# A decoder layer's RWKV recurrence: the inverse from its last row up, Pool's large operations on VectorE and ACT, the decay moved into the state update

## The chip, the core and the metric

The kernel runs on one core of a Trainium2 chip. Its engines work side by side, each through its own list of instructions in order: PE (TensorE, matrix products), DVE (VectorE), ACT (ScalarE), POOL (GpSimd) and SP, which here only issues DMAs. The metric is the device time of one execution in microseconds (us), lower is better.

## The reference

One step of one decoder layer for 512 prompt tokens and 8 sample tokens (520 columns, 2048 channels). What matters here is the RWKV-7 branch, a recurrence over time with one 64x64 state per head:

```python
kk = hd(k.astype(f32) * k_k)
kk = kk / jnp.maximum(jnp.sqrt(jnp.sum(kk * kk, axis=-1, keepdims=True)), 1e-12)
kf = hd(k.astype(f32) * (1.0 + (a - 1.0) * k_a))
...
def step(S, inp):
    r_t, w_t, k_t, v_t, a_t, b_t = inp
    sa = jnp.einsum('bhij,bhj->bhi', S, a_t)
    S = S * w_t[:, :, None, :] + sa[..., None] * b_t[:, :, None, :] + v_t[..., None] * k_t[:, :, None, :]
    return S, jnp.einsum('bhij,bhj->bhi', S, r_t)
...
S, o = _wkv7_scan(wkv_prev, rf, hd(decay), kf, vf, -kk, kk * hd(a))
```

`o` is normalised per head, a bonus term is added, and the sum is gated by `silu(gate_a)`. Beside it stands a convolution branch (31 taps, layer norm, its own gate). Both are projected, merged by sigmoid gates, projected again and normalised. All weights and activations are float32.

## The kernel before

**Matrix products.** Each large product takes its 128x512 weight block as a high and a low part: ACT copies the block rounded to `wh` (line 154), DVE subtracts, `wl = w - wh`, and PE runs three products of 260 columns for each half of the tokens (`step`, line 195; line 211). Four k-steps share one block, that is 24 matmuls. `wh` and `wl` have four buffers each, and a block is prepared three blocks ahead (`AHEAD`).

**The recurrence** is done in chunks of 64 tokens, for two heads (128 channels) at a time: eight passes of `wkv(p, box)`, p = 0 to 7. One pass has these stages:
- the prelude: `kk`, `b`, `kf` (kept in the tile named `a`), the bonus factor `rk`, its high part `hi`, the bonus `bv`, the decays `ep` and `em` (the latter in the tile `cs`), and the products `ar` and `bk` with them;
- the inverse: a 32x32 triangular matrix for each of 32 blocks, brought into `ni` through DRAM (`nd`), is inverted row by row, 31 times a multiply into `tm` and a sum into `ti`, both on DVE; the result goes through DRAM (`td`) into `tts`, DVE transposes a part of it to `d` (the program's `d11`), and two sets of small products on PE with `yt` between them complete the 64x64 inverse in `ttb`;
- the loop over 8 chunks: PE makes `aux`, ACT copies it to `xs`, PE multiplies by `ttb`, ACT copies to `suv`, PE multiplies by `bkt` (the transposed `bk`), and DVE makes the next state from `sf` and the chunk's decay `epl`; four k-steps of the large products stand between two such stages;
- the end: normalisation (`m`, `o`, `on`), `og`, and a DMA to `oa_d`.

The convolution of the same number (`conv(i, u)`: 30 multiply-adds of some 500 columns into `c` on DVE) runs after the inverse.

**Order.** The program writes PE's order, and for this part DVE's too. The stages above are generators that are advanced one tick after each k-step of a large product (`tick`, line 181). `yield n` waits n ticks. `yield ROOM` lets a stage go on only while a running sum of DVE's planned work is no more than 1 us ahead of PE's planned work. The sum charges a DVE instruction of n elements 0.14 + 0.00107 n us and a large Pool instruction 0.0007 n us; ACT's work is not charged. ACT, POOL and SP are ordered by the scheduler.

Nearly all DVE and POOL instructions are issued by one helper, so the profile gives them line 67; they are told apart by their tiles.

Of the kernel before, what the change touches and what calls it, by code (L numbers as in the profile page):

```python
# [70 lines left out]
def body(nc, tc, a):  # L71
    with ExitStack() as es:
# [356 lines left out]
        def wkv(p, box):  # L429
# [67 lines left out]
            yield 2
# [11 lines left out]
            ar = [kq.tile([P, NCH, 2, 64], F32, name=f"ar{h}", bufs=2) for h in range(2)]
            bk = kq.tile([P, NCH, 2, 64], F32, name="bk")  # L510
            for h in range(2):
                s = half(h)
                yield ROOM
                tt(vec, ar[h][s, :, h, :], ch(kk)[s], ep[s, :, 0:64], ALU.mult)
                tt(gps, ar[h][s, :, 1 - h, :], ch(r)[s], ep[s, :, 1:65], ALU.mult)
# [2 lines left out]
                tt(gps, bk[s, :, 1 - h, :], ch(kf)[s], ch(em)[s], ALU.mult)
# [37 lines left out]
            gps.tensor_copy(epl, ep[:, :, 64])  # L556
            tt(gps, bh, bh, ep[:, :, 64:65].to_broadcast([P, NCH, P]), ALU.mult)
            ni = kq.tile([P, 32, 32], F32, name="ni")
            for g in range(4):
# [4 lines left out]
            gps.tensor_scalar(ti.rearrange("p i t -> p (i t)"), ttinit, 1.0, 0.0, op0=ALU.mult, op1=ALU.add)
            yield 3
            for t in range(1, 32):
                tm = kq.tile([P, 8, 32], F32, name="tm")
                tt(vec, tm[:, :, :t + 1], ti[:, :, :t + 1],
                   ni[:, 0:t + 1, t].unsqueeze(1).to_broadcast([P, 8, t + 1]), ALU.mult)
                vec.tensor_reduce(ti[:, :, t], tm[:, :, :t + 1], axis=AX.X, op=ALU.add)  # L570
                yield ROOM
            flag["inv"] = p
            for g in range(4):
                dma(out=td.rearrange("h c e i t -> (h c e) i t")[:, g * 8:(g + 1) * 8, :], in_=ti[g * 32:(g + 1) * 32])
            for h in range(2):
                for e in range(2):
                    dma(out=tts[h * 64 + e * 32:h * 64 + e * 32 + 32, :, e * 32:e * 32 + 32],
                        in_=td[h, :, e].rearrange("c i t -> i c t"))
            yield 16
            for h in range(2):  # L580
# [19 lines left out]
            for c in range(NCH):  # L600
                for h in range(2):
                    x, y = quarter(2 * h), quarter(2 * h + 1)
                    pe.matmul(o[x, c, 0:32], lhsT=yt[y, c, :], rhs=tts[y, c, 32:64], start=True, stop=True)
            for h in range(2):
                s = half(h)
                gps.tensor_scalar(ttb[s, :, s], tts[s], 1.0, 0.0, op0=ALU.mult, op1=ALU.add)
# [21 lines left out]
            yield 7  # L628

            oc = aux("oc").rearrange("p (c x) -> p c x", x=64)  # L630
            sf = kq.tile([P, 64], F32, name="sf", bufs=2)
            gps.memset(sf, 0.0)
            for c in range(NCH):
                x = aux().rearrange("p (c x) -> p c x", x=64)
                for h in range(2):
                    pe.matmul(x[half(h), 0, :], lhsT=ar[h][:, c, h, :], rhs=suv[:, h, c, :], start=True, stop=True)
                for h in range(2):
                    pe.matmul(oc[half(h), c, :], lhsT=ar[h][:, c, 1 - h, :], rhs=suv[:, h, c, :], start=True, stop=False)
                xs = kq.tile([P, 64], F32, name="xs", bufs=2)
                act(xs, x[:, 0, :], AF.Copy)  # L640
                yield ly
                pe.matmul(x[:, 2, :], lhsT=ttb[:, c, :], rhs=xs, start=True, stop=True)
                for h in range(2):
                    act(suv[half(h), h, c, :], x[half(h), 2, :], AF.Copy)
# [42 lines left out]
            og = gt("og")[:, :NPR]  # L687
# [25 lines left out]
        def conv(i, u):  # L713

            yield 8
            sc = kp.tile([P, NS, 31], F32, name="sc")
# [13 lines left out]
            act(c[:, :NPR], u[:, :NPR], AF.Identity, scale=cw[:, 30:31], bias=col(O_CB, i))  # L730
# [400 lines left out]
```

## Time and profile before

| | |
|---|---|
| median of 3 runs | 1838.17 us (1833.41 to 1839.06) |
| the profiled execution's own time | 1836.85 us |
| its span, first to last instruction | 1835.1 us |
| PE busy | 1785.5 us (97%) |
| DVE busy | 1279.5 us (70%) |
| ACT busy | 743.3 us (41%) |
| POOL busy | 353.3 us (19%) |

The shares are means over a span whose stages differ: the eight passes of the recurrence fill about the first 1100 us, and what follows is the rest of the large products. `PEclk` is the clock that TensorE was granted, as a share of full speed. In a timeline, a number in square brackets is the idle time of the engine just before that instruction, with what ended it.

### The profile page before, as it was taken

Reading aid. Unit: us, or ns where it says so; the run is one execution under the profiler, and the core shown is the slowest. Engines: PE = TensorE matmul, PEld = TensorE weight load, DVE = VectorE, ACT = ScalarE, POOL = GpSimd, SP = SyncE. Lnnn points to the kernel's source line nnn. Section 1 sums busy time; section 2 is a strip of 40 time slices with the busy share of each in tenths; the row PEclk is TensorE's granted clock in tenths of the full one; section 3 lists DMA queues with packets and bytes.
Section 4 is the critical chain, followed back from the end, with each engine's and each line's share of the span. In section 5 each row is a group of like instructions: output and inputs, shape, how many; then the busy total and the mean of one; then the engine's idle time right before and its main releaser. Section 6 shows DMA issues by size and latency. Waiting matters only on the chain.

```text
span 1835.1 us, 37880 instructions
## 1 busy us (share of the span) xinstructions
PE 1785.5 (97%) x15576; PEld 1744.7 (95%) x15576; DVE 1279.5 (70%) x2300; ACT 743.3 (41%) x1355; POOL 353.3 (19%) x370
## 2 busy tenths in 40 slices
PE   9999999999999999999999999999999999999996
PEld 9999999999998999989999999999999999999995
DVE  6569999799798797896996998465444333334456
ACT  6735336244253363353362332454333222243354
POOL 1222203113113013032131155001022000011102
PEclk9999999999999999999999999999999999999998
DMA  6252322532432433324323344467555433362232
GB/s 232 84 133 79 107 93 79 114 92 74 119 103 68 112 96 98 96 80 107 94 84 104 122 131 149 130 225 238 192 179 185 123 116 98 93 195 93 93 104 94
DMA packets 121037, 220.49 MB, mean 120 GB/s; under 512 B 47888, under 2 KB 56208, under 8 KB 120864
## 3 DMA queue, kind: packets, MB, share of 16 engines
q1 hardware_dynamic: 119264, 216.47, 38.4%
q8 instruction: 122, 2.00, 0.4%
q10 hardware_dynamic: 1600, 1.60, 0.3%
q14 instruction: 51, 0.42, 0.1%
HBM read 188.69 MB, written 29.34 MB: 119 GB/s over the span
## 4 chain that ended last, share of the span: by engine, by line
PE 74%; DVE 19%; issue 3%; ACT 1%; POOL 1%; DMA 1%; SPq 0%; DVEq 0%; ACTq 0%; POOLq 0%
PE mm L211 68%; PE aux L67 5%; DVE wl L67 4%; DVE tm L67 4%; DVE c L67 3%; DVE ti L67 2%; PE aux L211 1%; DVE p L67 1%; DVE sq L67 1%; DVE on L67 1%; PE oc L67 1%; DMA w<-in_win 0%; DVE h L67 0%; DVE suv L67 0%; DVE m L67 0%
## 5 line engine op out<-in xcount | busy, mean ns | idle before, releaser
L154 ACT ACTIVATE wh<-w 128x512 fp32r<-128x512 f32 (+1 forms) x541 | 338.7, 628 | 627.5 <-PE mm L211 503.8
L211 PE MATMUL mm<-xh,wh 128*128 128x260 f32 x2784 | 589.1, 293 | 0.4 <-ACT xh L266 0.4
L211 PE MATMUL mm<-xh,wl 128*128 128x260 f32 x2784 | 565.9, 285 | 4.6 <-DVE wl L67 4.6
L211 PE MATMUL mm<-xl,wh 128*128 128x260 f32 x2784 | 566.0, 285 | 0.3 <-DVE xl L67 0.3
L67 DVE TENSOR_TENSOR wl<-w,wh 128x512 fp32r<-128x512 f32 (+1 forms) x541 | 397.5, 738 | 200.4 <-ACT wh L154 198.3
L211 PEld LDWEIGHTS mm<-xh,wh 128*128 128x128 f32 x2784 | 432.6, 191 | 12.1 <-ACT wh L154 0.6
L211 PEld LDWEIGHTS mm<-xh,wl 128*128 128x128 f32 x2784 | 433.7, 191 | 5.2 <-DVE wl L67 5.2
L211 PEld LDWEIGHTS mm<-xl,wh 128*128 128x128 f32 x2784 | 433.8, 191 | 0.6 <-DVE xl L67 0.5
L211 PE MATMUL mm<-hi,wl 128*128 128x260 f32 x1600 | 333.5, 284 | 2.6 <-DVE wl L67 2.6
L211 PE MATMUL mm<-hi,wh 128*128 128x260 f32 x1600 | 333.3, 283 | 0.0
L211 PE MATMUL mm<-lo,wh 128*128 128x260 f32 x1600 | 332.4, 282 | 0.0
L211 PEld LDWEIGHTS mm<-hi,wl 128*128 128x128 f32 x1600 | 250.7, 189 | 3.1 <-DVE wl L67 3.1
L211 PEld LDWEIGHTS mm<-hi,wh 128*128 128x128 f32 x1600 | 252.0, 189 | 0.1
L211 PEld LDWEIGHTS mm<-lo,wh 128*128 128x128 f32 x1600 | 251.8, 189 | 0.0
L67 DVE SCALAR_TENSOR_TENSOR c<-u,prm,c 128x482 f32<-128x482 f32 (+14 forms) x240 | 201.6, 840 | 4.4
L67 DVE TENSOR_TENSOR tm<-ti,ni 128x16 f32<-128x16 f32 (+30 forms) x248 | 104.1, 420 | 4.9
L67 POOL TENSOR_TENSOR sq<-hi,lo 128x520 f32<-128x520 f32 (+1 forms) x20 | 24.3, 1220 | 337.8 <-DVE one L67 184.0
L67 DVE TENSOR_TENSOR p<-mm,rs 128x520 f32<-128x520 f32 x78 | 53.7, 689 | 48.3 <-PE mm L211 48.2
L67 DVE TENSOR_REDUCE ti<-tm 128x8 f32<-128x16 f32 (+30 forms) x248 | 73.6, 297 | 8.5
L67 DVE TENSOR_TENSOR s<-mm,s 128x520 f32<-128x520 f32 x32 | 22.4, 700 | 65.9 <-PE mm L211 65.9
L67 POOL COPY nsh<-p 128x9 f32<-128x9 f32 x25 | 14.9, 597 | 238.0 <-DVE p L67 238.0
L67 DVE SCALAR_TENSOR_TENSOR suv<-sf,epl,aux 64x64 f32<-64x64 f32 x112 | 31.1, 278 | 38.4 <-PE aux L67 22.4
(233 smaller groups left out, 1652.5 us busy)
## 6 DMA issues: line engine op xcount, KB each, us to landing
w<-in_win SPq DMA_DIRECT2D x170, 512.0 KB, 3.7
w<-in_wout SPq DMA_DIRECT2D x32, 512.0 KB, 3.7
w<-in_wpg SPq DMA_DIRECT2D x24, 512.0 KB, 3.7
s<-sga_d SPq DMA_DIRECT2D x32, 260.0 KB, 2.8
w<-in_wpa SPq DMA_DIRECT2D x16, 512.0 KB, 3.8
w<-in_wpb SPq DMA_DIRECT2D x16, 512.0 KB, 3.8
wx<-in_wpg SPq DMA_DIRECT2D x32, 256.0 KB, 3.5
x<-in_xT SPq DMA_DIRECT2D x16, 260.5 KB, 5.7
```

What stands on the lines that cost most here:

```text
L67: return f(*args, **kw)
L154: behind.append(act(wh[:, k], w[:, k], AF.Copy))
L211: nc.tensor.matmul(o[h], lhsT=w[:, used[0] % 4, :], rhs=x[:, h * HF:(h + 1) * HF], start=(k == 0 and i == 0), stop=(k == nk - 1 and i == 2))
```

## The change

1. The inverse runs from row 30 up to row 0 and multiplies by `ni[:, t:t+1, t:]`, a row of each matrix, where the old one multiplied by a column `ni[:, 0:t+1, t]`. The result comes out in the other orientation: it is loaded as `dtt`, used by PE directly for the first set of small products, and transposed once on DVE to `dt` for the second.
2. Pool's large operations of the recurrence move. To DVE: the half of `ar` and `bk` that Pool made, the product `kf*k`, the two products of `og` (the first now reads PE's result and applies the scale), and in the convolution the samples' product `tm` and the sum `csum`. To ACT: `kf`'s scale and offset, the bias of `og` (now added to `bv`), `epl`, the initial `ti`, and the copies into `ttb`.
3. The product of all of `bk` with the chunk's last decay (`bh`, 128x1024 on Pool) goes. The decay is applied in the state update instead: DVE makes `suv = aux*epl + sf`, and ACT makes the next `sf` from it by a scale. The separate DVE instruction for `sf` stays for the last chunk only.
4. `og` uses the buffer of `bv`, and `rk` of pass p waits in the program until `og` of pass p-2 was issued (`flag["out"]`).

```diff
-            gps.tensor_scalar(kf, av, col(O_KA, p), oka[:, p:p + 1], op0=ALU.mult, op1=ALU.add)
-            tt(gps, kf, kf, k, ALU.mult)
-            yield 5
+            act(kf, av, AF.Identity, scale=col(O_KA, p), bias=oka[:, p:p + 1])
+            yield 3
+            tt(vec, kf, kf, k, ALU.mult)
+            yield 1
...
+            while p > 1 and flag["out"] < p - 2:
+                yield 1
...
+            act(bv[:, :NPR], bv[:, :NPR], AF.Identity, bias=col(O_LB, p))
...
-                tt(gps, ar[h][s, :, 1 - h, :], ch(r)[s], ep[s, :, 1:65], ALU.mult)
+                yield ROOM
+                tt(vec, ar[h][s, :, 1 - h, :], ch(r)[s], ep[s, :, 1:65], ALU.mult)
...
-            tt(gps, bh, bh, ep[:, :, 64:65].to_broadcast([P, NCH, P]), ALU.mult)
...
-            gps.tensor_scalar(ti.rearrange("p i t -> p (i t)"), ttinit, 1.0, 0.0, op0=ALU.mult, op1=ALU.add)
+            act(ti.rearrange("p i t -> p (i t)"), ttinit, AF.Copy)
...
-            for t in range(1, 32):
+            for t in range(30, -1, -1):
                 tm = kq.tile([P, 8, 32], F32, name="tm")
-                tt(vec, tm[:, :, :t + 1], ti[:, :, :t + 1],
-                   ni[:, 0:t + 1, t].unsqueeze(1).to_broadcast([P, 8, t + 1]), ALU.mult)
-                vec.tensor_reduce(ti[:, :, t], tm[:, :, :t + 1], axis=AX.X, op=ALU.add)
+                tt(vec, tm[:, :, t:], ti[:, :, t:], ni[:, t:t + 1, t:].to_broadcast([P, 8, 32 - t]), ALU.mult)
+                vec.tensor_reduce(ti[:, :, t], tm[:, :, t:], axis=AX.X, op=ALU.add)
...
-                vec.transpose(d11[h * 64:h * 64 + 32], tts[h * 64:h * 64 + 32, :, 0:32])
+            vec.transpose(dt, dtt)
...
-                    pe.matmul(o[y, c, 0:32], lhsT=nba[x, c, 32:64], rhs=d11[x, c, :], start=True, stop=True)
+                    pe.matmul(o[y, c, 0:32], lhsT=nba[x, c, 32:64], rhs=dtt[x, c, :], start=True, stop=True)
...
-                        vec.scalar_tensor_tensor(suv[s, h, c + 1, :], sf[s], epl[s, c:c + 1], x[s, 3, :], op0=ALU.mult, op1=ALU.add)
-                s0 = sf
-                sf = kq.tile([P, 64], F32, name="sf", bufs=2)
-                vec.scalar_tensor_tensor(sf, s0, epl[:, c:c + 1], x[:, 3, :], op0=ALU.mult, op1=ALU.add)
+                        vec.scalar_tensor_tensor(suv[s, h, c + 1, :], x[s, 3, :], epl[s, c:c + 1], sf[s], op0=ALU.mult, op1=ALU.add)
...
+                    act(sf[half(h)], suv[half(h), h, c + 1, :], AF.Copy, scale=epl[half(h), c + 1:c + 2])
...
-            act(og, ot, AF.Identity, scale=col(O_LG, p), bias=col(O_LB, p))
-            tt(gps, og, og, bv[:, :NPR], ALU.add)
-            tt(gps, og, og, sl[:, :NPR], ALU.mult)
+            yield 1
+            vec.scalar_tensor_tensor(og, ot, col(O_LG, p), bv[:, :NPR], op0=ALU.mult, op1=ALU.add)
+            tt(vec, og, og, sl[:, :NPR], ALU.mult)
```

PE's instructions keep their number and sizes, and so do the loads and stores around the inverse (four `td` stores, four loads back). Two places show how the lists move. The first is DVE in the prelude of one pass while the loop of the pass ahead runs; `c` is the convolution, `wl` the weights' low part. Before:

```order
L67 SCALAR_TENSOR_TENSOR kk<-kk,sq 128x520
L67 SCALAR_TENSOR_TENSOR b<-kk,a 128x520
L67 TENSOR_TENSOR wl<-w,wh 128x512
L67 SCALAR_TENSOR_TENSOR c<-u,prm,c 128x505
L67 SCALAR_TENSOR_TENSOR c<-u,prm,c 128x506
L67 SCALAR_TENSOR_TENSOR c<-u,prm,c 128x507
L67 TENSOR_TENSOR wl<-w,wh 128x512
L67 SCALAR_TENSOR_TENSOR rk<-r,prm,a 128x520
```

And now:

```order
L67 SCALAR_TENSOR_TENSOR kk<-kk,sq 128x520
L67 SCALAR_TENSOR_TENSOR b<-kk,a 128x520
L67 SCALAR_TENSOR_TENSOR c<-u,prm,c 128x507
L67 TENSOR_TENSOR wl<-w,wh 128x512
L67 SCALAR_TENSOR_TENSOR c<-u,prm,c 128x508
L67 TENSOR_TENSOR a<-a,k 128x520
L67 SCALAR_TENSOR_TENSOR c<-u,prm,c 128x509
L67 TENSOR_TENSOR wl<-w,wh 128x512
L67 SCALAR_TENSOR_TENSOR rk<-r,prm,a 128x520
```

The product `a*k` stands on DVE between `b` and `rk`, so `rk` waits for nothing on Pool any more. The second place is ACT at the end of an inverse, where the initial `ti` of the next pass is now made. Before, with `ti` on Pool's list:

```order
L674 ACTIVATE m<-m,eps 128x8
L154 ACTIVATE wh<-w 128x512
L154 ACTIVATE wh<-w 128x512
L154 ACTIVATE wh<-w 128x512
L689 ACTIVATE og<-aux,prm 128x512
L382 ACTIVATE q<-p,prm 128x519
L154 ACTIVATE wh<-w 128x512
```

And now:

```order
L679 ACTIVATE m<-m,eps 128x8
L154 ACTIVATE wh<-w 128x512
L154 ACTIVATE wh<-w 128x512
L567 ACTIVATE ti<-cst 128x256
L154 ACTIVATE wh<-w 128x512
L382 ACTIVATE q<-p,prm 128x519
L154 ACTIVATE wh<-w 128x512
```

`ti` may be overwritten only when the four `td` stores of the pass that has just ended have read it, so on ACT the following conversions of weights and the next `q` now stand behind that wait; `og` has left ACT.

More of the change, by code (lines that the diff above doesn't have):

```diff
@@ L408, in lowrank @@
             flag["low"] = True
-        tts = kq.tile([P, NCH, 64], F32, name="tts")
         ttb = kq.tile([P, NCH, P], F32, name="ttb")
         nbrs = [kq.tile([P, NCH, P], F32, name=f"nbr{i}") for i in range(2)]
-        for x in (tts, ttb, *nbrs):
+        for x in (ttb, *nbrs):
             gps.memset(x, 0.0)
-        d11 = kq.tile([P, NCH, 32], F32, name="d11")
-        flag = {"samples": 0, "inv": -1, "done": -1, "loop": -1, "conv": 0, "yp": None, "merged": False}
+        flag = {"samples": 0, "out": -1, "inv": -1, "done": -1, "loop": -1, "conv": 0, "yp": None, "merged": False}
         def firsts(box):
@@ L514, in wkv @@
                 tt(vec, ar[h][s, :, h, :], ch(kk)[s], ep[s, :, 0:64], ALU.mult)
[L515 removed]
+                yield ROOM
+                tt(vec, ar[h][s, :, 1 - h, :], ch(r)[s], ep[s, :, 1:65], ALU.mult)
                 yield ROOM
                 tt(vec, bk[s, :, h, :], ch(b)[s], ch(em)[s], ALU.mult)
[L518 removed]
+                yield ROOM
+                tt(vec, bk[s, :, 1 - h, :], ch(kf)[s], ch(em)[s], ALU.mult)
             for i, x in enumerate((kk, b, kf, r, v)):
@@ L555, in wkv @@
             epl = kq.tile([P, NCH], F32, name="epl", bufs=2)
-            gps.tensor_copy(epl, ep[:, :, 64])
-            tt(gps, bh, bh, ep[:, :, 64:65].to_broadcast([P, NCH, P]), ALU.mult)
+            act(epl, ep[:, :, 64], AF.Copy)
             ni = kq.tile([P, 32, 32], F32, name="ni")
@@ L574, in wkv @@
                 dma(out=td.rearrange("h c e i t -> (h c e) i t")[:, g * 8:(g + 1) * 8, :], in_=ti[g * 32:(g + 1) * 32])
+            dtt = kq.tile([P, NCH, 32], F32, name="dtt")
             for h in range(2):
                 for e in range(2):
[L577 to L580, printed above, removed]
-                vec.transpose(d11[h * 64:h * 64 + 32], tts[h * 64:h * 64 + 32, :, 0:32])
+                    dma(out=dtt[h * 64 + e * 32:h * 64 + e * 32 + 32], in_=td[h, :, e].rearrange("c t i -> t c i"))
+            yield 18
+            dt = kq.tile([P, NCH, 32], F32, name="dt")
+            vec.transpose(dt, dtt)
             yield 4
@@ L602, in wkv @@
                     x, y = quarter(2 * h), quarter(2 * h + 1)
[L603 to L606, printed above, removed]
+                    pe.matmul(o[x, c, 0:32], lhsT=yt[y, c, :], rhs=dt[y, c, :], start=True, stop=True)
+            for q in map(quarter, range(4)):
+                act(ttb[q, :, q], dt[q], AF.Copy)
             for h in range(2):
@@ L630, in wkv @@
             oc = aux("oc").rearrange("p (c x) -> p c x", x=64)
-            sf = kq.tile([P, 64], F32, name="sf", bufs=2)
-            gps.memset(sf, 0.0)
+            sf = kq.tile([P, 64], F32, name="sf")
             for c in range(NCH):
@@ L649, in wkv @@
                     pe.matmul(oc[half(h), c, :], lhsT=nbr[:, c, h * 64:h * 64 + 64], rhs=suv[:, h, c, :], start=False, stop=True)
-                if c + 1 < NCH:
-                    for h in range(2):
-                        s = half(h)
-                        vec.scalar_tensor_tensor(suv[s, h, c + 1, :], sf[s], epl[s, c:c + 1], x[s, 3, :], op0=ALU.mult, op1=ALU.add)
-                s0 = sf
-                sf = kq.tile([P, 64], F32, name="sf", bufs=2)
-                vec.scalar_tensor_tensor(sf, s0, epl[:, c:c + 1], x[:, 3, :], op0=ALU.mult, op1=ALU.add)
+                for h in range(2) if c + 1 < NCH else ():
+                    s = half(h)
+                    if c:
+                        vec.scalar_tensor_tensor(suv[s, h, c + 1, :], x[s, 3, :], epl[s, c:c + 1], sf[s], op0=ALU.mult, op1=ALU.add)
+                    else:
+                        vec.tensor_scalar(suv[s, h, 1, :], x[s, 3, :], epl[s, 0:1], None, op0=ALU.mult)
+                for h in range(2) if c + 1 < NCH else ():
+                    act(sf[half(h)], suv[half(h), h, c + 1, :], AF.Copy, scale=epl[half(h), c + 1:c + 2])
+                if c + 1 == NCH:
+                    vec.scalar_tensor_tensor(sf, x[:, 3, :], epl[:, c:c + 1], sf, op0=ALU.mult, op1=ALU.add)
                 yield ly
@@ L686, in wkv @@
                 pe.transpose(ot[:, c * P:(c + 1) * P], on[:, c, :], ident)
-            og = gt("og")[:, :NPR]
+            og = bv[:, :NPR]
             sl = box["sl"]
-            act(og, ot, AF.Identity, scale=col(O_LG, p), bias=col(O_LB, p))
-            tt(gps, og, og, bv[:, :NPR], ALU.add)
-            tt(gps, og, og, sl[:, :NPR], ALU.mult)
+            yield 1
+            vec.scalar_tensor_tensor(og, ot, col(O_LG, p), bv[:, :NPR], op0=ALU.mult, op1=ALU.add)
+            tt(vec, og, og, sl[:, :NPR], ALU.mult)
             dma(out=oa_d[p, :, 0:NPR], in_=og)
+            flag["out"] = p
         def gnorm(o, og, n):
@@ L725, in conv @@
             tm = et("tm")[:, :NS * 31].rearrange("p (b k) -> p b k", k=31)
-            tt(gps, tm, sc, cw.unsqueeze(1).to_broadcast([P, NS, 31]), ALU.mult)
             yield 5
+            yield ROOM
+            tt(vec, tm, sc, cw.unsqueeze(1).to_broadcast([P, NS, 31]), ALU.mult)
             vec.tensor_reduce(c[:, NPR:], tm, axis=AX.X, op=ALU.add)
@@ L739, in conv @@
             if i == 0:
-                gps.tensor_scalar(csum, c, 1.0, 0.0, op0=ALU.mult, op1=ALU.add)
+                act(csum, c, AF.Copy)
             else:
-                tt(gps, csum, csum, c, ALU.add)
+                tt(vec, csum, csum, c, ALU.add)
             flag["conv"] += 1
```

## The prediction

> **What bounds the kernel now.** I read the windows first, then what PE waited for, then the timelines around those waits.
>
> Busy time by stage; the columns are PE, its weight loads, DVE, ACT, POOL, then the granted clock, DMA share and GB/s:
>
> ```profile
> 250.00:300.00 50.00, 48.02 (x453) 46.00 (x453) 48.47 (x91) 27.95 (x55) 6.27 (x16) 0.97 0.27 81
> 550.00:600.00 50.00, 47.02 (x410) 44.78 (x409) 39.37 (x66) 18.01 (x36) 19.27 (x18) 0.93 0.29 80
> 750.00:800.00 50.00, 46.47 (x421) 45.26 (x420) 46.36 (x86) 19.07 (x38) 8.12 (x14) 0.93 0.31 99
> 800.00:850.00 50.00, 48.48 (x425) 46.32 (x424) 43.62 (x69) 25.34 (x46) 15.71 (x17) 0.97 0.25 79
> 900.00:950.00 50.00, 47.98 (x437) 46.70 (x436) 47.29 (x76) 30.37 (x52) 8.98 (x16) 0.93 0.32 100
> 1050.00:1100.00 50.00, 48.37 (x443) 46.89 (x444) 46.22 (x57) 15.19 (x34) 25.73 (x17) 0.93 0.45 143
> 1200.00:1250.00 50.00, 50.00 (x419) 50.00 (x418) 33.57 (x54) 26.89 (x44) 1.69 (x1) 1.00 0.65 215
> ```
>
> From 1200 us on PE is busy in all 50.00 us of a window at full clock: nothing on DVE or POOL can be gained there. In these windows of the recurrence PE loses 1.5 to 3.5 us, DVE is busy 39 to 48 us, and the clock falls to 0.93 or 0.97. PE's waits (total, times, longest), one of ACT's, and two places:
>
> ```profile
> PE aux L67 <- DVE d L67: 8.9, 11, 2.2
> PE mm L211 <- DVE wl L67: 7.2, 5, 2.4
> PE aux L67 <- ACT suv L644: 5.5, 2, 3.0
> PE aux L67 <- ACT xs L640: 4.1, 3, 1.9
> PE aux L67 <- DVE suv L67: 3.4, 2, 1.8
> PE aux L67 <- ACT yt L591: 2.5, 3, 2.2
> ...
> ACT hi L361 <- DVE rk L67: 30.2, 7, 6.4
> ...
> 1069.56 0.50 PE L211 MATMUL mm<-xh,wl 128*128 128x260 f32 x2 [1.42 <-DVE wl L67]
> 1803.79 0.39 PE L211 MATMUL mm<-hi,wl 128*128 128x260 f32 x1 [2.39 <-DVE wl L67]
> ```
>
> Of `wl`'s 7.2 us, 2.4 lie at 1803 us, in the tail, which the change doesn't touch. So PE idles 8.9 + 4.8 + 5.5 + 4.1 + 3.4 + 2.5 = 29 us in the recurrence. The clock costs more: the six windows shown below 1.00 lack 0.03 + 0.07 + 0.07 + 0.03 + 0.07 + 0.07 = 0.34 of 50 us, 17 us. Together 46 us is all that this change can win.
>
> Why DVE is late shows in one stretch (start, duration, engine):
>
> ```profile
> 814.84 0.62 DVE L67 TENSOR_TENSOR wl<-w,wh 128x512 fp32r<-128x512 f32 x1
> ...
> 817.69 1.67 DVE L67 SCALAR_TENSOR_TENSOR b<-kk,a 128x520 f32<-128x520 f32 x1
> 819.28 1.68 DVE L67 TENSOR_TENSOR wl<-w,wh 128x512 fp32r<-128x512 f32 x1
> 820.88 3.63 DVE L67 SCALAR_TENSOR_TENSOR c<-u,prm,c 128x506 f32<-128x506 f32 x3
> 824.44 1.78 DVE L67 TENSOR_TENSOR wl<-w,wh 128x512 fp32r<-128x512 f32 x1
> 826.14 1.78 DVE L67 SCALAR_TENSOR_TENSOR rk<-r,prm,a 128x520 f32<-128x520 f32 x1
> ...
> 827.95 0.64 ACT L361 ACTIVATE hi<-rk 128x520 fp32r<-128x520 f32 x1 [4.55 <-DVE rk L67]
> ...
> 817.62 2.79 POOL L67 TENSOR_TENSOR ar<-r,ep 64x512 f32<-64x512 f32 x2 [3.10 <-ACT ep L480]
> 820.52 1.59 POOL L67 TENSOR_SCALAR a<-a,prm,oka 128x520 f32<-128x520 f32 x1
> 824.05 3.31 POOL L67 TENSOR_TENSOR bk<-a,cs 64x512 f32<-64x512 f32 x2
> ```
>
> The same `wl` takes 0.62 us with POOL idle and 1.68 to 1.78 us while POOL runs a large operation; `b`, `rk` and the convolution are stretched alike. ACT, in order, stands 4.55 us before `hi<-rk` here and 30.2 us in seven passes, and the chunk loop's `xs` and `suv` stand behind it. That is where PE's waits for `suv` and `xs` come from. The other part of DVE's lateness:
>
> ```profile
> L67 DVE TENSOR_TENSOR tm<-ti,ni 128x16 f32<-128x16 f32 (+30 forms) x248 | 104.1, 420 | 4.9
> L67 DVE TENSOR_TENSOR tm<-ti,ni 128x256 f32<-128x256 f32 x8 | 5.0, 624 | 0.0
> L67 DVE TENSOR_TENSOR tm<-ti,ni 128x16 f32<-128x16 f32 x8 | 1.4, 170 | 0.0
> L67 DVE TENSOR_TENSOR lorl<-lor,lorh 128x256 fp32r<-128x256 f32 x8 | 3.3, 418 | 0.0
> L67 DVE SCALAR_TENSOR_TENSOR c<-u,prm,c 128x482 f32<-128x482 f32 (+14 forms) x240 | 201.6, 840 | 4.4
> L67 DVE SCALAR_TENSOR_TENSOR c<-u,prm,c 128x482 f32<-128x482 f32 x8 | 5.7, 717 | 0.1
> L67 DVE SCALAR_TENSOR_TENSOR v<-p,omu,q 128x520 f32<-128x520 f32 x8 | 6.0, 750 | 0.1
> L67 DVE SCALAR_TENSOR_TENSOR rk<-r,prm,a 128x520 f32<-128x520 f32 x8 | 12.9, 1610 | 3.3 <-POOL a L67 3.2
> ```
>
> A `tm` that reads a column of `ni` takes 624 ns for 256 elements; a multiply of that size with contiguous operands takes 418. The planner charges 0.14 + 0.00107 x 256 = 414 ns. So DVE falls behind its plan in each inverse and each convolution, and PE, whose order was laid by that plan, waits for `d`, `wl` and `yt` at the end of the inverse.
>
> **The change part by part.** PE's matmuls and the DMAs keep number and size: no cost.
>
> *The inverse by rows.* 248 `tm` keep their sizes, 136 elements in the mean. Between 170 ns at 16 elements and 418 at 256, a contiguous one of 136 takes about 295 ns. DVE saves 248 x (420 - 295) = 31 us, 3.9 us a pass. The bounds: nothing (if the column isn't what costs) and these 31 us. I take 31, since the row of 418 has the operands of the new form but for a repeat of the row. One transpose of 128x256 stands for two of 32x256 (a half us saved each pass), and PE no longer waits for it: the first small products read what the DMA brought.
>
> *The operations moved to DVE.* These rows price them, and ACT's:
>
> ```profile
> L67 DVE TENSOR_TENSOR ar<-aux,cst 64x512 f32<-64x512 f32 x32 | 22.0, 688 | 0.4
> L67 DVE SCALAR_TENSOR_TENSOR sf<-sf,epl,aux 128x64 f32<-128x64 f32 x64 | 17.9, 280 | 6.9 <-PE aux L67 5.1
> L640 ACT ACTIVATE xs<-aux 128x64 f32<-128x64 f32 x64 | 14.3, 223 | 56.8 <-PE aux L67 56.4
> L730 ACT ACTIVATE c<-u,prm 128x512 f32<-128x512 f32 x8 | 6.5, 816 | 6.6 <-DMA c_d<-c 3.0 <-DVE u L67 2.7 <-DMA w<-in_win 0.7
> ```
>
> Each pass gains seven multiplies of about 0.69 (two `ar`, two `bk`, `kf*k`, `og*sl`, `csum`), one of 0.75 for `og` from PE's result and one of 0.42 for the samples' `tm`: 6.0 us, 48 us over eight passes. Removed: 56 of 64 `sf`, 56 x 0.28 = 16 us. With the 31 and the 4 us of transposes, DVE's own work changes by 48 - 16 - 31 - 4 = -3 us: nothing, by itself.
>
> *What POOL's absence gives DVE.* The convolution's 240 instructions average 840 ns, where the undisturbed rows give 717 to 750: 735 x 240 = 176, so 25 us are stretch. `rk` adds 8 x (1.61 - 0.75) = 7. In the stretch above `b` loses 0.9 and two `wl` 1.1 each, 25 us if every pass were like it; I take half, 12: 44 us together. POOL keeps three gate products a pass and the samples' products after 1050 us; I let a quarter of the stretch stay and take 33 us. The bounds are 0 and 44. DVE then has 36 us less in the eight passes, 4.5 us each.
>
> *ACT* gains 112 scales of `sf` at 0.22 (25 us). By the line from 223 ns for 64 elements to 816 for 512, one of 256 takes 0.48: each pass gains 4 copies to `ttb` and `ti` of that size, `kf` and `bv` at 0.82, `epl` 0.2, less `og` 0.82, 3.4 us. That is 25 + 27 = 52 us in eight passes, 6.5 us each, where ACT is busy 15 to 30 of 50 us. Its cover is that idle time, and weights are prepared three blocks ahead.
>
> *The waits.* `hi<-rk` should wait for 1 to 2 us instead of 4.3 in the mean (30.2 over 7) and 6.4 at most, as `rk` takes 0.75 and waits for no POOL operation; new on ACT are `kf` behind `b`, the bias behind `bv`, `sf` behind `suv` and `ti` behind the `td` stores. Behind each stand weights with a lead of blocks, and `xs` with four k-steps (2.9 us) before PE wants it; I price them at 0 to 8 us together, and take 3. The wait of `rk` for `flag["out"]` holds back pass 2 alone, by five ticks, off PE's path.
>
> *The sum.* Of the 46 us, the 1.4 at 1069 us and the drop of clock beside it (3.5) stay, as the samples' products stay on POOL. For the rest I compare DVE's excess over the plan in inverse and convolution, per pass: now 31 x (420 - 286 planned) + 30 x (840 - 672) = 4.2 + 5.0 = 9.2 us; after, 31 x 9 + 30 x (735 to 770 - 672) = 2.2 to 3.2. A quarter to a third stays, and of 41 us I leave a sixth, 7, since PE's waits begin only past the slack of the plan, and 3 for ACT. Gain 46 - 5 - 7 - 3 = 31 to 36 us; I take 34. The profiled execution ran 1836.85 us for a span of 1835.1 and lies 1.3 below the median; by it 1803, by the median 1838.2 - 34 = 1804. I say 1804.
>
> [...] The trace has the drops in windows with idle and full clock at 1200 us, where there is none, so I take them as won with the gaps.
>
> **The rivals.**
>
> *Nearly all of it goes* (chance 0.18): DVE stays inside the plan everywhere, and only the samples' 5 us remain: 1838 - 41 = 1797. For it: DVE's planned and true costs then agree within 3 us a pass.
>
> *Half* (0.20): one family of waits stays, the clock with it, or the clock's drops don't hang on the gaps: 1838 - 20 = 1818. Against the last: the drops' windows are those with idle.
>
> *Nothing moves* (0.10): the stretch is not POOL's doing, or returns as DVE's own 48 us of added work. Then DVE keeps its load (-3 us), the waits stay, and the time is 1836. Against it: 0.62 and 1.68 for the same `wl` within 5 us, with POOL's start between.
>
> *ACT's `ti` blocks* (0.07), the one that ends slower. Where POOL held this instruction it stood up to 16 us before the stores had landed:
>
> ```profile
> 771.87 0.42 DVE L67 TENSOR_REDUCE ti<-tm 128x8 f32<-128x256 f32 x1
> 777.61 0.41 POOL L67 TENSOR_SCALAR ti<-cst 128x256 f32<-128x256 f32 x1 [16.14 <-DMA td<-ti]
> ```
>
> If ACT came as early, PE would run through its four `wh` blocks, 4 x 24 matmuls at 50/419 = 0.119 us, 11.5 us, less 1.4 for conversion and `wl`: 6 us of idle and 1.7 of clock in each of seven passes, 54 us, and the time 1838 - 34 + 54 = 1858. It decides from 34/7 = 5 us a pass, that is a wait of ACT past 13 us. Against it: `ti` stands between two `wh` which wait for PE's buffers, so ACT comes there about when the inverse ends, and 777.61 is 5.3 us after its last sum. [...]
>
> **How the numbers follow.** My forecast, 1804 give or take 6, has 0.45; the rivals 0.18, 0.20, 0.10 and 0.07. From 1790 (all 46 us and a little) to 1822 lie the forecast, the first two rivals and little else, 0.8 and a bit. 0.3% is 5.5 us, about what a measurement of this kernel can tell from no change. Faster by more: 0.45 + 0.18 + 0.20 + a little of the fourth = 0.85; the same 0.08; slower 0.07.
>
> **What would show it.** Right: PE's wait for `d` gone (no such tile) and none of 2 us for `dtt`; `hi<-rk` waiting under 2 us; `tm` near 300 ns in the mean, the convolution under 780, `rk` near 750 to 850; POOL far under its 353 us, ACT near 743 + 52 = 795, DVE near 1280 - 36 = 1244; the clock at 1.00 in nearly all windows up to 1050 us. Wrong: `tm` still at 420 (the column doesn't cost), the convolution still at 840 (POOL doesn't stretch it), or PE waiting for `xs`, `yt` or `wh` behind ACT's `ti`, `kf` or `bv`.

## The result, and the profile after

| | before | after |
|---|---|---|
| median | 1836.59 us (1833.41 to 1839.06, 4 runs) | 1790.66 us (1790.24 to 1793.13, 4 runs) |
| the profiled execution, its span | 1836.85, 1835.1 us | 1790.92, 1789.1 us |
| PE, DVE, ACT, POOL busy | 1785.5, 1279.5, 743.3, 353.3 us | 1765.2, 1231.2, 809.2, 198.0 us |

The ratio of the times is 0.9754, 95% interval 0.9734 to 0.9773: faster by 45.9 us. 1790.66 lies at the lower end of the range given (1790 to 1822), outside the forecast's own 1804 give or take 6, and nearest to the rival "nearly all of it goes" (1797).

The windows of the changed kernel, with the columns as in the prediction (PE, its weight loads, DVE, ACT, POOL, granted clock, DMA share, GB/s):

```profile
250.00:300.00 50.00, 50.00 (x493) 48.19 (x492) 43.23 (x86) 32.81 (x65) 3.13 (x11) 1.00 0.29 90
300.00:350.00 50.00, 48.95 (x448) 46.32 (x446) 45.21 (x82) 21.21 (x47) 6.01 (x6) 1.00 0.36 97
550.00:600.00 50.00, 50.00 (x462) 47.86 (x461) 34.15 (x82) 19.72 (x46) 5.72 (x6) 1.00 0.42 105
750.00:800.00 50.00, 50.00 (x487) 48.63 (x486) 45.63 (x76) 34.71 (x65) 4.72 (x10) 1.00 0.28 88
900.00:950.00 50.00, 50.00 (x459) 47.62 (x458) 39.66 (x73) 24.77 (x51) 4.75 (x8) 1.00 0.34 101
1000.00:1050.00 50.00, 46.57 (x451) 44.46 (x450) 47.40 (x60) 18.48 (x42) 21.34 (x15) 1.00 0.48 149
```

The clock is 1.00 in each, and PE is busy in all of its time in four of the six. The window at 300 us loses 1.05 us, and the one at 1000 us, with the samples' products on POOL (21.34 us busy), 3.43. What PE waits for, in total, times and longest:

```profile
PE mm L211 <- DVE wl L67: 3.8, 3, 2.4
PE aux L1046 <- ACT sq L1035: 1.9, 1, 1.9
PE aux L67 <- ACT suv L645: 1.7, 1, 1.7
PE aux L254 <- DVE zero L67: 1.2, 1, 1.2
PE aux L67 <- DVE lo L67: 0.8, 1, 0.8
PE aux L67 <- ACT xs L641: 0.4, 1, 0.4
```

The waits for `d`, `yt` and the state `suv` from DVE are gone; `sq` and 2.4 of `wl` lie in the tail, `zero` at the start. The groups that answer to those of before (busy, mean ns, idle before and what ended it):

```profile
L67 DVE TENSOR_TENSOR tm<-ti,ni 128x16 f32<-128x16 f32 (+30 forms) x248 | 79.1, 319 | 5.5
L67 DVE SCALAR_TENSOR_TENSOR c<-u,prm,c 128x482 f32<-128x482 f32 (+14 forms) x240 | 183.9, 766 | 4.4
L67 DVE SCALAR_TENSOR_TENSOR rk<-r,prm,a 128x520 f32<-128x520 f32 x8 | 6.0, 755 | 0.0
L67 DVE TENSOR_TENSOR a<-a,k 128x520 f32<-128x520 f32 x8 | 5.6, 698 | 10.7 <-ACT a L486 10.7
L361 ACT ACTIVATE hi<-rk 128x520 fp32r<-128x520 f32 x8 | 5.1, 639 | 7.0 <-DVE rk L67 7.0
L567 ACT ACTIVATE ti<-cst 128x256 f32<-128x256 f32 x8 | 3.3, 411 | 1.1 <-DMA td<-ti 0.7 <-DVE wl L67 0.3
L659 ACT ACTIVATE sf<-suv,epl 64x64 f32<-64x64 f32 x112 | 38.7, 346 | 53.4 <-DVE suv L67 51.7
L645 ACT ACTIVATE suv<-aux 64x64 f32<-64x64 f32 x128 | 27.5, 215 | 60.5 <-PE aux L67 58.9
```

`tm` fell from 420 to 319 ns, the convolution from 840 to 766, `rk` from 1610 to 755, ACT's wait before `hi<-rk` from 30.2 to 7.0 us. ACT stood 1.1 us in all before `ti`, so the rival that would have ended slower did not come.

**An account of the loss.** Below, "idle" is the sum of PE's idle stretches between 20 and 1200 us (the bracketed numbers of the timelines), and "clock" is half the time in which the records show TensorE at half its clock there. Before it was 29.3 + 17.1 us, after 4.5 + 0. That accounts for 41.9 of 45.9 us; the other 4 us are not found in these two sums (PE's busy time fell by 20.3 us, 3 more than the clock explains).

### The profile page after: what moved, and what is told of

Same layout as the page of the kernel before. It is cut to its first block, busy times and chain, and to the rows that moved or that the text cites. A ratio compares the mean times of both kernels' runs of the same rounds, so it can differ in the third digit from the quotient of the medians.

```text
span 1789.1 us, 37790 instructions
## 1 busy us (share of the span) xinstructions
PE 1765.2 (99%) x15576; PEld 1727.6 (97%) x15576; DVE 1231.2 (69%) x2307; ACT 809.2 (45%) x1528; POOL 198.0 (11%) x241
## 4 chain that ended last, share of the span: by engine, by line
PE 95%; DVE 4%; issue 1%; ACT 0%; DMA 0%; SPq 0%; DVEq 0%
PE mm L211 87%; PE aux L67 6%; DVE c L67 1%; PE aux L211 1%; DVE wl L67 1%; PE oc L67 1%; DVE h L67 0%; DMA w<-in_wfst 0%; DVE p L67 0%; DVE bv L67 0%; DVE on L67 0%; DVE rf L67 0%; DVE m L67 0%; ACT L1028 0%; PE aux L1046 0%
## 5 line engine op out<-in xcount | busy, mean ns | idle before, releaser
L211 PE MATMUL mm<-xh,wh 128*128 128x260 f32 x2784 | 583.0, 291 | 0.0
L67 DVE TENSOR_TENSOR wl<-w,wh 128x512 fp32r<-128x512 f32 (+1 forms) x541 | 379.9, 706 | 198.0 <-ACT wh L154 195.7
L211 PEld LDWEIGHTS mm<-xh,wh 128*128 128x128 f32 x2784 | 427.5, 188 | 11.5 <-ACT wh L154 0.5
L211 PEld LDWEIGHTS mm<-xh,wl 128*128 128x128 f32 x2784 | 427.9, 188 | 1.9 <-DVE wl L67 1.8
L211 PEld LDWEIGHTS mm<-xl,wh 128*128 128x128 f32 x2784 | 428.3, 188 | 0.8 <-DVE xl L67 0.8
L67 DVE SCALAR_TENSOR_TENSOR c<-u,prm,c 128x482 f32<-128x482 f32 (+14 forms) x240 | 183.9, 766 | 4.4
L67 DVE TENSOR_TENSOR tm<-ti,ni 128x16 f32<-128x16 f32 (+30 forms) x248 | 79.1, 319 | 5.5
L67 DVE SCALAR_TENSOR_TENSOR suv<-aux,epl,sf 64x64 f32<-64x64 f32 x96 | 27.2, 283 | 59.3 <-PE aux L67 56.8
L659 ACT ACTIVATE sf<-suv,epl 64x64 f32<-64x64 f32 x112 | 38.7, 346 | 53.4 <-DVE suv L67 51.7
```

What stands on the lines that cost most here:

```text
L67: return f(*args, **kw)
L211: nc.tensor.matmul(o[h], lhsT=w[:, used[0] % 4, :], rhs=x[:, h * HF:(h + 1) * HF], start=(k == 0 and i == 0), stop=(k == nk - 1 and i == 2))
L659: act(sf[half(h)], suv[half(h), h, c + 1, :], AF.Copy, scale=epl[half(h), c + 1:c + 2])
```

## The experiments

Each kernel was timed together with the kernel before, on the same chip; "gain" is the difference of the two medians there (the kernel before had 1836.19 to 1838.56 us). The last column is DVE's busy time.

| kernel | median us | gain us | ratio, 95% interval | idle + clock us | DVE us |
|---|---|---|---|---|---|
| before | 1836.59 | | | 29.3 + 17.1 | 1279.5 |
| after | 1790.66 | 45.9 | 0.9754 (0.9734 to 0.9773) | 4.5 + 0 | 1231.2 |
| rows_only | 1799.12 | 37.1 | 0.9799 (0.9782 to 0.9815) | 8.3 + 1.7 | 1249.5 |
| moves_only | 1807.16 | 29.2 | 0.9833 (0.9814 to 0.9851) | 14.5 + 1.7 | 1265.5 |
| decay_only | 1826.60 | 9.6 | 0.9946 (0.9929 to 0.9963) | 26.7 + 8.5 | 1268.9 |
| col_read | 1804.67 | 31.5 | 0.9832 (0.9813 to 0.9851) | 12.7 + 1.7 | 1259.9 |
| decay_back | 1795.20 | 43.4 | 0.9769 (0.9755 to 0.9784) | 6.6 + 1.7 | 1241.5 |
| pool_sets | 1791.29 | 45.1 | 0.9751 (0.9737 to 0.9766) | 4.4 + 0 | 1230.4 |
| pool_one | 1817.56 | 21.0 | 0.9884 (0.9869 to 0.9900) | 17.6 + 10.2 | 1272.4 |
| pool_reads | 1828.08 | 8.3 | 0.9948 (0.9933 to 0.9963) | 26.9 + 8.5 | 1279.3 |
| pool_back | 1817.64 | 18.6 | 0.9898 (0.9862 to 0.9934) | 19.7 + 11.9 | 1246.1 |
| pool_back_ttb | 1814.07 | 24.5 | 0.9867 (0.9850 to 0.9883) | 17.9 + 3.4 | 1248.2 |
| halves_back | 1795.30 | 41.6 | 0.9772 (0.9758 to 0.9787) | 7.0 + 0 | 1239.5 |
| ak_back | 1788.63 | 48.2 | 0.9735 (0.9719 to 0.9752) | 2.5 + 0 | 1233.8 |

### Each part alone: rows_only, moves_only, decay_only

rows_only is the kernel before with the first part of the change:

```diff
-            for t in range(1, 32):
-                tt(vec, tm[:, :, :t + 1], ti[:, :, :t + 1],
-                   ni[:, 0:t + 1, t].unsqueeze(1).to_broadcast([P, 8, t + 1]), ALU.mult)
+            for t in range(30, -1, -1):
+                tt(vec, tm[:, :, t:], ti[:, :, t:], ni[:, t:t + 1, t:].to_broadcast([P, 8, 32 - t]), ALU.mult)
```

> The kernel before with the inverse by rows alone (and the two loads, the transpose and the ttb copies that go with it; POOL keeps everything). tm from 420 to about 320 ns, DVE about 1250 us, the wait for d gone (8.9 us). Theory: 1805 to 1822 us, the waits of hi<-rk as before (about 30 us), the clock still below 1.00 in two to four windows. Rival 'the rows alone carry it': 1790 to 1798. Rival 'POOL alone': 1833 to 1838.

Measured: a gain of 37.1 us, between the theory's range and the rival's. `tm` took 318 ns and no wait for `d` is left. But ACT still stood 24.7 us before `hi<-rk`, and the convolution was as slow as before:

```profile
L67 DVE SCALAR_TENSOR_TENSOR c<-u,prm,c 128x482 f32<-128x482 f32 (+14 forms) x240 | 205.6, 857 | 4.4
L361 ACT ACTIVATE hi<-rk 128x520 fp32r<-128x520 f32 x8 | 5.1, 637 | 27.9 <-DVE rk L67 24.7 <-POOL og L67 3.2
```

So these two can go on almost unchanged without costing PE much, once DVE has 25 us less to do in the inverses. rows_only also takes a transpose out of PE's way, as PE's first small products now read the loaded `dtt` and no longer wait for `d`; how the 37.1 us divide between this and the shorter `tm` isn't shown.

moves_only is the changed kernel with the column inverse and the product on `bh` as before; only the moves from POOL to DVE and ACT are left.

```diff
+            tt(gps, bh, bh, ep[:, :, 64:65].to_broadcast([P, NCH, P]), ALU.mult)
...
-            for t in range(30, -1, -1):
+            for t in range(1, 32):
```

> The changed kernel with the inverse by columns and the decay on bh as before: only the moves from POOL to DVE and ACT are left. DVE keeps tm at 420 ns and gets 48 us of moved work, less what it is stretched. Theory (column and POOL each for a part; rows alone gave 37 of 46 us): 1812 to 1828 us, hi<-rk waits under 2 us, d or dtt still waited for. Rival 'POOL alone is enough as well': 1791 to 1805. Rival 'the moves only load DVE': 1834 to 1845.

Measured: 1807.16, a gain of 29.2 us, more than the theory's 1812 to 1828 allowed and less than "POOL alone is enough" said. DVE was busy for 1265.5 us, 14 less than before, though it had taken over seven multiplies a pass. PE still waited 5.2 us for `dt` at the end of the inverse.

decay_only is the kernel before with the third part alone:

```diff
-            tt(gps, bh, bh, ep[:, :, 64:65].to_broadcast([P, NCH, P]), ALU.mult)
...
-                        vec.scalar_tensor_tensor(suv[s, h, c + 1, :], sf[s], epl[s, c:c + 1], x[s, 3, :], op0=ALU.mult, op1=ALU.add)
+                        vec.scalar_tensor_tensor(suv[s, h, c + 1, :], x[s, 3, :], epl[s, c:c + 1], sf[s], op0=ALU.mult, op1=ALU.add)
```

> The kernel before with the decay in the state update alone: bh's product (15 us on POOL) gone, 56 of 64 sf on DVE (16 us) replaced by 112 scales on ACT at about 0.35 us. Theory: a small part, 1824 to 1835 us; tm stays at 420 ns, hi<-rk waits on. Rival 'the shorter chain in the loop carries it' (PE's waits for suv and xs, 9.6 us, and the clock with them): 1805 to 1818.

Measured: a gain of 9.6 us, as the theory had it; PE still waited 11.0 us for `suv` from ACT.

The three gains make 37.1 + 29.2 + 9.6 = 75.9 us, where the whole change brings 45.9. The parts take away some of the same waits, so their gains don't add. A kernel with the rows and the decay together, rows_decay, has no time, as it deadlocks; what this pair brings is open.

### Each part taken back: col_read, decay_back

col_read is the changed kernel that reads `ni` by column in the same order and sizes; what the inverse computes is then not the inverse, and only the address pattern is put back.

```diff
-                tt(vec, tm[:, :, t:], ti[:, :, t:], ni[:, t:t + 1, t:].to_broadcast([P, 8, 32 - t]), ALU.mult)
+                tt(vec, tm[:, :, t:], ti[:, :, t:], ni[:, t:, t].unsqueeze(1).to_broadcast([P, 8, 32 - t]), ALU.mult)
```

> The changed kernel, in which the 31 multiplies of each inverse read a column of ni again, in the same order and sizes (so the inverse's numbers are wrong: only the address pattern is put back). Theory (both the column and POOL made DVE late, each for a part): tm back from 319 to about 420 ns, DVE 1231 + 25 = 1256 us, 3.1 us a pass of lateness again, and a part of PE's idle at the inverse's end comes back: 1796 to 1810 us. Rival 'POOL alone': with POOL quiet DVE has the slack for it, 1790 to 1793. Rival 'the column alone': nearly all comes back, 1820 to 1835.

```profile
L67 DVE TENSOR_TENSOR tm<-ti,ni 128x16 f32<-128x16 f32 (+30 forms) x248 | 106.6, 430 | 5.5
```

430 ns against 319, with nothing changed but the addresses: the column costs 111 ns an instruction, 27.5 us in all, and the time rose by 14.4 us (gain 31.5 instead of 45.9). The theory's range held (1804.67 in 1796 to 1810).

decay_back is the changed kernel with `bh`'s product on POOL and `sf` on DVE as before.

> The changed kernel with the decay on bh (one product of 128x1024 on POOL a pass) and sf on DVE as before; rows and moves stay. POOL up by 15 us, DVE by 16 us, ACT less by 39 us. Theory (by now DVE is inside its plan, so the decay's 10 us are not to be had twice): 1789 to 1794 us. Rival (the state's chain counts by itself): 1798 to 1803 us.

Measured 1795.20, a gain of 43.4, 2.5 us less than the whole change: between the theory (1789 to 1794) and the rival (1798 to 1803), nearer to the theory. Alone the decay brought 9.6 us; the 2.5 beside the others can't be told from nothing, as the two intervals overlap.

### What on POOL disturbs DVE: pool_reads, pool_sets, pool_one

These three add work to POOL in the changed kernel, at one place in each pass, right after `epl`. Nothing uses its result, no plan charges it, and DVE and ACT get nothing to do but one small copy on ACT in two of them.

```diff
             act(epl, ep[:, :, 64], AF.Copy)
+            for _ in range(10):     # pool_reads
+                nc.gpsimd.tensor_tensor(scr, cst[:, 0:448].rearrange("p (c t) -> p c t", t=56), epl.unsqueeze(2).to_broadcast([P, NCH, 56]), op=ALU.mult)
+            for _ in range(28):     # pool_sets
+                nc.gpsimd.memset(scr, 0.0)
+            for _ in range(20):     # pool_one
+                nc.gpsimd.tensor_scalar(scr, cst[:, 0:448].rearrange("p (c t) -> p c t", t=56), 1.0, 0.0, op0=ALU.mult, op1=ALU.add)
```

> The changed kernel with ten products of 128x448 on POOL added in each pass, right after epl is made, whose result nothing uses and which no plan charges: about 80 x 1.35 = 108 us on POOL, no new work for DVE. Theory (a POOL product stretches what DVE does beside it, and that reaches PE in part): POOL about 305 us, DVE up by 20 to 45 us at the same number of instructions, 1794 to 1806 us. Rival 'POOL matters only by results that DVE and ACT wait for' (rk behind a*k): 1789 to 1793.

> The changed kernel with 28 memsets of 128x448 on POOL added in each pass at the same place, which read nothing: about 224 x 0.45 = 100 us on POOL. If it is POOL's reading that stretches DVE, DVE stays near 1231 us, the convolution near 766 ns, and the time 1789 to 1793 us. If any POOL operation does it, DVE rises as with the added products and the time too.

> The changed kernel with 20 copies of 128x448 on POOL added in each pass at the place of the added products and memsets: one operand read from memory instead of two (the products cost 37 us of time, the memsets, which read none, nothing). About 160 x 0.6 = 96 us on POOL. Theory 'every read stretches DVE': DVE between 1231 (memsets) and 1279 us (products), about 1250, and 1797 to 1815 us. Rival 'only two operands at once do': DVE near 1231 and 1789 to 1793 us.

The groups of the added work, from the three kernels in this order:

```profile
L562 POOL TENSOR_TENSOR scr<-cst,epl 128x448 f32<-128x448 f32 x80 | 99.5, 1244 | 56.6 <-ACT epl L560 51.2
```

```profile
L563 POOL MEMSET scr<- 128x448 f32 x224 | 105.8, 472 | 64.0 <-ACT scr L561 52.7
```

```profile
L563 POOL TENSOR_SCALAR scr<-cst 128x448 f32<-128x448 f32 x160 | 133.2, 832 | 64.4 <-ACT scr L561 53.0
```

99.5 us of products undid 37.6 of the 45.9 us, more than twice the most that the theory allowed (1806 us, some 15 lost). 105.8 us of memsets at the same place undid 0.8, which is nothing. 133.2 us of copies with one operand undid 24.9, just past the theory's range, with DVE at 1272 us where the theory had 1250. One stretch of the first two shows it (start, duration, engine). The products:

```profile
317.05 2.73 DVE L67 SCALAR_TENSOR_TENSOR c<-u,prm,c 128x496 f32<-128x496 f32 x2
318.00 6.58 POOL L562 TENSOR_TENSOR scr<-cst,epl 128x448 f32<-128x448 f32 x5
319.71 1.42 DVE L67 TENSOR_TENSOR wl<-w,wh 128x512 fp32r<-128x512 f32 x1
321.05 4.07 DVE L67 SCALAR_TENSOR_TENSOR c<-u,prm,c 128x498 f32<-128x498 f32 x3
```

The memsets:

```profile
313.00 7.90 POOL L563 MEMSET scr<- 128x448 f32 x15
...
313.81 0.75 DVE L67 SCALAR_TENSOR_TENSOR rk<-r,prm,a 128x520 f32<-128x520 f32 x1
314.48 0.73 DVE L67 SCALAR_TENSOR_TENSOR c<-u,prm,c 128x501 f32<-128x501 f32 x1
315.14 0.68 DVE L67 TENSOR_TENSOR wl<-w,wh 128x512 fp32r<-128x512 f32 x1
```

Beside products a `wl` takes 1.42 us, beside memsets 0.68. DVE's own instructions were the same 2307 in all three, and its busy time went from 1231.2 to 1279.3, 1230.4 and 1272.4 us: a POOL busy with memsets, which read nothing, did not stretch DVE, one busy with products or copies, which read, did. The `ar<-aux,cst`, which read one operand from PE's result, stayed at 688 to 689 ns in every kernel. Few of them met the added work (2 of 32 in pool_reads), but in the kernel before nine stood wholly beside products on POOL and took 694 ns, against 686 for those beside nothing. So with one operand from PE an instruction took 8 ns more beside products, while a `wl`, with none from PE, took 0.74 us more there (1.42 against 0.68).

### Part by part back on POOL: pool_back, pool_back_ttb, ak_back, halves_back

pool_back is the changed kernel with `kf`, the halves of `ar` and `bk`, and the two operations of `og` on POOL again.

```diff
-            act(kf, av, AF.Identity, scale=col(O_KA, p), bias=oka[:, p:p + 1])
-            tt(vec, kf, kf, k, ALU.mult)
+            gps.tensor_scalar(kf, av, col(O_KA, p), oka[:, p:p + 1], op0=ALU.mult, op1=ALU.add)
+            tt(gps, kf, kf, k, ALU.mult)
...
-                tt(vec, ar[h][s, :, 1 - h, :], ch(r)[s], ep[s, :, 1:65], ALU.mult)
+                tt(gps, ar[h][s, :, 1 - h, :], ch(r)[s], ep[s, :, 1:65], ALU.mult)
...
-            tt(vec, og, og, sl[:, :NPR], ALU.mult)
+            tt(gps, og, og, sl[:, :NPR], ALU.mult)
```

> The changed kernel with kf's scale and product, the halves of ar and bk and the two sums and products of og on POOL again (og's scale on ACT), as before. POOL's busy time rises from 198 to about 300 us, DVE issues 48 instructions fewer (about 33 us less work of its own) but is stretched. Theory: rk waits for POOL's a*k again, hi<-rk waits 3 to 4 us in each pass, the convolution rises from 766 to about 810 ns, the time is 1798 to 1815 us. Rival 'the rows alone carried it': 1788 to 1793. Rival 'POOL alone': 1820 to 1836.

Measured 1817.64: 27.4 us of the gain gone, just past the theory's range. Its four runs lie apart, two at 1814 us and two at 1821 and 1825, so the loss is known to some 7 us only; the profile is of the run at 1821. DVE was busy for only 1246.1 us, 3 less than in rows_only, which was 18.5 us faster. Here the place seems to count, not the sum. PE stood five times at `suv`, for 1.35 to 2.77 us, and five times for more than 1 us at `yt`, for 1.04 to 1.61. One of each (start, duration, engine; the bracket is the idle time before):

```profile
556.95 3.35 POOL L67 TENSOR_TENSOR bk<-a,cs 64x512 f32<-64x512 f32 x2
557.35 1.79 DVE L67 TENSOR_TENSOR wl<-w,wh 128x512 fp32r<-128x512 f32 x1
559.06 1.79 DVE L67 SCALAR_TENSOR_TENSOR rk<-r,prm,a 128x520 f32<-128x520 f32 x1
...
563.50 0.59 DVE L67 SCALAR_TENSOR_TENSOR suv<-aux,epl,sf 64x64 f32<-64x64 f32 x2
...
563.83 0.59 PE L67 MATMUL aux<-suv,ar 128*64 128x64 f32 x3 [1.41 <-DVE suv L67]
```

```profile
524.29 1.26 ACT L605 ACTIVATE ttb<-dt 32x256 f32<-32x256 f32 x3
...
525.58 0.78 ACT L591 ACTIVATE yt<-aux 32x256 f32<-32x256 f32 x2
...
526.01 0.24 PE L67 MATMUL aux<-dt,yt 32*32 32x32 f32 x2 [1.34 <-ACT yt L591]
```

`wl` and `rk` lose 2.1 us to POOL's two `bk` (1.79 each instead of 0.68 and 0.75), and `suv` stands behind them on DVE. On ACT three copies into `ttb` stand ahead of `yt`. pool_back_ttb puts these copies on POOL:

```diff
-                act(ttb[q, :, q], dt[q], AF.Copy)
+                gps.tensor_scalar(ttb[q, :, q], dt[q], 1.0, 0.0, op0=ALU.mult, op1=ALU.add)
```

> The kernel with the large operations back on POOL, and the four copies from dt into ttb on POOL too instead of ACT (as in the kernel with the rows alone). In it PE waited 8.2 us for yt, 11 times, with the copies ahead of yt on ACT. Theory 'the copies on ACT hold up yt': those waits and the clock drops behind them go, 1803 to 1809 us. Rival 'ACT comes late for other reasons': 1814 to 1820 us, with yt still waited for.

PE's wait for `yt` fell from 8.2 to 2.2 us, as expected, but the time only to 1814.07, at the edge of the rival's range and inside the spread of pool_back's own runs: `suv` went on at 9.2 us. So a gain from this move isn't shown. The other two put back one piece each, with the same lines as above.

> The changed kernel with only kf's scale and the product a*k back on POOL (two operations a pass, 24 us in all), so that rk waits for POOL again. Everything back on POOL had cost 27 us. If it is the late rk (hi<-rk, and behind it xs and suv on ACT) that carries it: 1806 to 1816 us and hi<-rk waiting over 20 us. If it is the stretch beside the halves of ar and bk: 1791 to 1796 us, hi<-rk 10 to 15 us.

> The changed kernel with only the halves of ar and bk back on POOL (four products of 64x512 a pass, 48 us in all); a*k stays on DVE, so that rk waits for nothing on POOL. If the stretch beside POOL's products carries it: rk and the convolution stretched, 1800 to 1815 us. If it is rk's wait for a*k: 1790 to 1796 us.

ak_back missed both ways: it is no slower than the changed kernel, rather 2 us faster (1788.22 to 1788.96 in its runs against 1790.24 to 1793.13; the intervals of the ratios overlap). ACT waited 14.0 us before `hi<-rk`, twice as long as after, and PE did not notice. halves_back lost 4.3 us, though `rk` was stretched to 1407 ns. Its 1795.30 lies in the range that was given for `rk`'s wait for `a*k`, but ak_back rules this cause out. So neither `a*k` nor the halves carry the 27 us: alone they cost -2.3 and 4.3, and both intervals overlap that of the changed kernel. The loss comes with them together and with `og`; a kernel with `og` alone on POOL wasn't run, and which of them do it is open. The faster rows_only differs from pool_back by the third part of the change and the small moves; rows_decay would have told these apart. In the profiled run 11.9 us are the clock, which halves_back didn't lose at all.

## Why the prediction was right, and where not

- *What bounds.* Right: the gain lies in the recurrence. At the 9600th of PE's 15576 instructions (1101.4 us before, 1055.7 after) the changed kernel leads by 45.7 us, at the last by 45.9. That 46 us were counted as lost and 45.9 were won is partly chance, as 4.5 us of idle stay and 4 us of the gain are in neither idle nor clock.
- *The inverse by rows.* `tm` 319 ns instead of 295: 25 us on DVE instead of 31. The line through the sizes was right, with 300 ns for 136 elements. What it left out is POOL's product `gb`, which stays: in five of the eight passes one `tm` stood beside it and took 1.09 to 1.27 us instead of 0.2, some 20 ns in the mean of all 248. col_read shows that the column was the cause of the rest of the old 420 ns. In the changed kernel, the size that met `gb` four times, the size of mean length, and one such place (start, duration, engine):

```profile
L67 DVE TENSOR_TENSOR tm<-ti,ni 128x56 f32<-128x56 f32 x8 | 5.9, 739 | 0.2
L67 DVE TENSOR_TENSOR tm<-ti,ni 128x136 f32<-128x136 f32 x8 | 2.4, 300 | 0.2
...
594.47 0.20 DVE L67 TENSOR_TENSOR tm<-ti,ni 128x48 f32<-128x48 f32 x1
...
594.84 1.31 POOL L67 TENSOR_TENSOR gb<-p,sg 128x520 f32<-128x520 f32 x1 [14.70 <-ACT sg L396]
594.95 1.27 DVE L67 TENSOR_TENSOR tm<-ti,ni 128x56 f32<-128x56 f32 x1
```

- *The moves.* Predicted at 0.69 us each; `ar`, `bk`, `a*k` and `og*sl` measured 682 to 700 ns. Right.
- *What POOL's absence gives DVE.* Mis-sized, too low. The convolution gained 17.7 us (840 to 766), `rk` 6.9, and `wl`, of which I had taken two a pass and then half, 17.6 us (397.5 to 379.9 over 541; alone it takes 0.68 us, and the 0.62 that I read off was among the shortest). DVE fell by 48.3 us to 1231.2, where I had 36 and 1244. That it is POOL's reading that stretches DVE is shown by pool_reads, pool_sets and pool_one (DVE at 1279.3, 1230.4 and 1272.4 us, for 1231.2 without the added work).
- *ACT.* 809.2 us instead of 795: the 112 scales of `sf` took 346 ns, not 220, 14 us more. This cost PE nothing that the waits show.
- *The waits.* `hi<-rk` 7.0 us over 7, at most 1.6; `ti` 1.1 in all. Right. But the step that said "that is where PE's waits for `suv` and `xs` come from" gave `hi<-rk` too large a part: rows_only kept 24.7 us of this wait and ak_back 14.0, and PE's idle fell to 8.3 and 2.5 us all the same.
- *What stays.* This term failed, and with it the time came out 13 us under the forecast: I left 5 + 7 + 3 = 15 us and took 34 of 46. Measured were 4.5 us idle and no clock loss. The "sixth of 41" treated the waits as a share of DVE's excess. The runs show that they end almost wholly with a part of the relief (rows_only: 37.1 us for 30 us of DVE), so that "DVE stays inside its plan", the rival at 1797, was the better reading of my own 2.2 to 3.2 us a pass. At the samples, where I left 1.4 us and a drop of 3.5, 3.4 us of idle stay and no drop.
- *The clock.* Right: I took the drops as won with the gaps, and all seven before 1200 us went with them: 17.1 us, without which the result would have been near 1808. The 1.7 us of clock that a pass was charged under *ACT's `ti` blocks* are half of the 3.413 us that the shortest drops last in the trace before.

## What to carry to other kernels

Where a kernel's order is laid by planned costs, gains of several parts need not add, as they can take away the same lateness: measure each alone and taken back before trusting a sum (here 75.9 against 45.9 us). An operation on GpSimd that reads memory wasn't free here though GpSimd idled (99.5 us of products cost 37.6 us of time, 105.8 us of memsets 0.8): count what DVE does beside it, where no operand is PE's result, at about double its time (0.68 us became 1.42 to 1.79 beside products), and move it, or make it one that only writes. A wait in an engine's list (ACT's `hi<-rk`) is a cause only if the bound engine's idle goes with it; a run that keeps the wait and loses the idle settles that.

## What the runs showed of the hardware

**The clock fell to half behind gaps of 1.34 us and more, but not behind each.** In the kernel before, around the gap at 264 us (PE's matmuls; the second number is the duration of a row's group):

```profile
261.94 0.40 PE L211 MATMUL mm<-xh,wl 128*128 128x260 f32 x2
264.19 0.59 PE L67 MATMUL aux<-suv,ar 128*64 128x64 f32 x3 [1.84 <-DVE suv L67]
...
265.98 0.64 PE L211 MATMUL mm<-xh,wh 128*128 128x260 f32 x2
266.42 0.64 PE L211 MATMUL mm<-xl,wh 128*128 128x260 f32 x2
...
268.91 0.41 PE L211 MATMUL mm<-xl,wh 128*128 128x260 f32 x2
```

Two matmuls take 0.40 us before the gap, 0.64 for some 3 us after it, and then 0.41 again: the profile records half the clock from 265.34 to 268.75 us, right behind a gap of 1.84 us. In the records of all kernels the spells before 1200 us last 3.413 us or twice that, and within a kernel they start at whole multiples of 3.413 us from one another. Gaps from 1.34 us on (pool_back, at 526 us) had a drop behind them.

Other gaps had none: four of 1.50 to 1.57 us in pool_back_ttb, one of 2.56 before, at 440 us, and one of 3.12 in decay_only, at 1062 us. Where a gap lies on that grid counts: in the kernel before, of two gaps of 1.84 us the one that ends at 264.19 lies within one window of 3.413 us and has a drop behind it, and the one that ends at 402.00 falls into two, as 1.71 and 0.13, and has none. Take PE's idle between 20 and 1200 us in the 14 traces and sum it by windows of each kernel's grid: of the windows at full clock, none with less than 1.41 us of idle was followed by a drop, and all 14 with 1.80 us or more were. Of those between, 19 were and 20 weren't, so what decides there stays open. A drop of one such length costs 1.7 us, about as much as the gap.

**A scale read from a column.** ACT's `sf<-suv,epl` took 346 ns, its `suv<-aux` of the same 64x64 without such an operand 215; the two also differ in where they read from. For the column read on DVE the cost is clear, as only the addresses changed: 0.8 ns an element (111 ns over 136 elements).
